# A hybrid decoder block: the inverse joined later, groups begun earlier, first products amid the transposes

## The chip, the cores and the metric

The kernel runs on one core of a Trainium2 chip. The metric is the device time of one execution in microseconds (us). TensorE is PE below, VectorE DVE, ScalarE ACT, GpSimd POOL and SyncE SP.

## The reference, cut to what matters

One layer over 2048 tokens of width 1024, all in float32. Half of the mixing heads are RWKV-7 time mixing (8 heads of 64), the other half differential attention (4 heads); then an output projection, and an MLP with a short causal convolution.

```python
xn = rms_norm(h, ln_attn_pre);  proj = xn @ w_in            # 1792 RWKV and 1536 attention columns
# RWKV, per head: r, k, v, decay, a, g from proj mixed with the token before
kk = k * k_k;  kk = kk / max(norm(kk), 1e-12)               # the key norm
state = state * w + (state @ -kk) (kk * a)^T + v k^T        # token after token
y = state @ r;  y = layer_norm(y + sum(r * k * r_k) * v) * g
o = differential attention of the other columns
h = h + rms_norm(concat(y, o) @ w_out)
h = h + rms_norm((gelu(conv(hn @ w_up)[gate]) * conv(...)[val]) @ w_down)
```

## The kernel before, in words

The run has four stages: projections with the RWKV groups between them; attention; output projection; MLP. The change lies in the first, apart from one buffer count in attention.

**Projections.** The tokens are handled in two halves of 1024, each in two runs `g` of 512. A column block `cb` has 128 columns: 14 blocks for RWKV, 12 for attention. Each float32 operand is split into a high part (rounded) and a low part (the rest), and a product of a block and a run is 24 matmuls of 128x512: three for each of 8 slices of the contraction (L270 to L272). `norm` (L181) loads 128 tokens of x, scales them and stores them as `xn`; `transpose_half` (L85) transposes 512 of their columns on PE (L89), ACT copies the high part (L91) and DVE makes the low part (L92). `start` does this for the first half and then issues the products of blocks 0 and 1. For the second half, `turn` loads `xn` back and transposes it. `plan` yields the other products: blocks 2 to 13 of the first half, then all of the second, then the attention blocks of the first. `evict` writes each product to DRAM, the RWKV blocks as `rw`.

**Pace.** `Pace` is a queue of generators. Each of the 8 steps of a product is one tick, three matmuls; after it, every generator whose tick has come is advanced to its next `yield`, which names the tick, counted from its own start, at which it goes on. So the order on PE is written by hand; inside `manual_schedule` PE's instructions run in the order of the program. The other engines and the DMA queues are ordered by a planner, which runs the program in a modelled time; each engine then runs its list in order.

**A group** (`Rwkv.group`, L449) is 128 tokens of time mixing in two chunks of 64. 16 groups start `PITCH` = 34 ticks apart. In its order:

- Loads by SP; at tick 5 the decay and rate products (L475, L477).
- At 8 the sums of squares of the keys (L492), then `power` (DVE L434, POOL L435); at 13 the eight rows of norms are turned on PE (L441) and split into high and low (L442 on ACT, L443 on DVE); at 16 PE spreads them (L447), and DVE finishes the keys (L518 to L524).
- At 22 and 24 the chunk products `M` (L540, masked by DVE at L543).
- The inverse: M's diagonal 32x32 blocks go to DRAM and back as `ab` (L548, L552), DVE runs 31 steps of two instructions each (L594, L596) on `X`, and X goes through DRAM (`xdr`, L599) to `x1t` (L601), `bdx` and M. `bda` holds M's blocks off the diagonal (L559). At tick `JOIN` = 52 PE joins the blocks: L618 reads `x1t`, L624 `bda`, L628 `bdx`, with an ACT copy after each.
- From `JOIN` + 7 the state: per chunk L643 (state times keys), three ticks later L649, three later L657 to L665, and DVE's update of the state (L662, L663).
- 21 ticks after that the output norm: sums (L675, L682), `power`, turning, spreading, and the gate (L695).

All PE outputs of this stage share 8 PSUM banks in turn.

Of the kernel before, what the change touches and what calls it, by code (L numbers as in the profile page):

```python
# [18 lines left out]
P = 128  # L19
# [3 lines left out]
HALF = 1024  # L23
GRP = 512
NRW = 14
# [9 lines left out]
def load_table(nc, cx, pool, eng, rows, name):  # L35


    tot = sum(r.shape[0] for r in rows)
    st = pool.tile([P, P], F32, name=f"{name}_st", tag=f"tab_st{name}")
    o = 0  # L40
    nc.vector.memset(st, 0.0)
    for r in rows:
        eng.dma_start(st[o:o + r.shape[0], :], r)
        o += r.shape[0]

    def finish():
        pt = cx.ps.tile([P, P], F32, name=f"{name}_ps", tag=cx.mm[0], bufs=cx.mm[1])
        nc.tensor.transpose(pt, st, cx.ident)
        t = cx.const.tile([P, tot], F32, name=name, tag=name)
        nc.vector.tensor_copy(t, pt[:, :tot])  # L50
        return t
    return finish
# [25 lines left out]
def transpose_split(nc, cx, ps, xn, xh, xl, t, tag, bufs):  # L78

    g, o = divmod(t * P, GRP)  # L80
    for hf in range(2):
        transpose_half(nc, cx, ps, xn[:, hf * 512:hf * 512 + 512], xh[g], xl[g], t, hf, o, tag, bufs)
# [75 lines left out]
class Proj:  # L158
# [10 lines left out]
        self.x, self.w = {}, {}  # L169

    def tables(self):
        nc, cx, I = self.nc, self.cx, self.I
        cols = lambda a: a.rearrange("(b p) -> b p", p=P)
        tab = load_table(nc, cx, self.pool, nc.sync, [cols(I["mu_shift"][0]), I["diff_subln"]]
                         + [cols(I[n][0]) for n in self.rk] + [cols(I["r_k"][0].rearrange("h d -> (h d)"))], "chtab")()
        self.mu, cx.subln = tab[:, 0:NRW], tab[:, NRW:NRW + 1]
        cx.rktab = {n: tab[:, NRW + 1 + 4 * i:NRW + 5 + 4 * i] for i, n in enumerate(self.rk + ["r_k"])}
        self.mu1 = cx.const.tile([P, NRW], F32, name="mu1")
        nc.vector.tensor_scalar(self.mu1, self.mu, -1.0, 1.0, op0=ALU.mult, op1=ALU.add)

    def norm(self, t, pool):  # L181

        nc = self.nc
        xt = pool.tile([P, D], F32, name=f"x_{t}", tag="xt", bufs=8)
        nc.sync.dma_start(xt, self.I["x"][0, t * P:(t + 1) * P, :])
        if self.gain is None:
            self.gain = bcast_row(nc, pool, self.I["ln_attn_pre"], D, "g_pre", nc.sync)
        norm_rows(nc, self.cx, pool, xt, xt, self.gain, t)
        nc.sync.dma_start(self.cx.xn[t], xt)
        return xt  # L190

    def alloc(self, half, g):
# [2 lines left out]
        self.x[half, g] = mk("h"), mk("l")  # L195
        return self.x[half, g]

    def start(self, first):

        cx = self.cx  # L200
        xs = [self.alloc(0, g) for g in range(2)]
        for t in range(HALF // P):
            if t == W0:
                self.weights(0, 0)
            if t == TB:
                self.tables()
            transpose_split(self.nc, cx, cx.ps, self.norm(t, first), [x[0] for x in xs], [x[1] for x in xs], t, *cx.ra)
        self.weights(0, 1)
        for g in range(2):
            for cb in range(2):  # L210
                self.product(0, cb, g)
# [113 lines left out]
NC = RG // 64  # L325
MB, SB = 2, 2
ARB = 3
PITCH, JOIN = 34, 52
NGRP = S // RG
DECAY = math.exp(-0.5)  # L330
LN_EPS = 64e-5
# [85 lines left out]
class Rwkv:  # L417
# [20 lines left out]
    def turned(self, bank, sb, rT):  # L438
        nc, cx = self.nc, self.cx
        tp = bank[0:8, 1, :]  # L440
        nc.tensor.transpose(tp, sb, cx.ident)  # L441
        nc.scalar.copy(rT[0:8], tp)  # L442
        nc.vector.tensor_tensor(rT[32:40], tp, rT[0:8].bitcast(F32), op=ALU.subtract)  # L443

    def spread(self, bank, rT):
# [3 lines left out]
    def group(self, g):  # L449
        tc, nc, cx, T, U = self.env(g)  # L450
# [35 lines left out]
        cum = T([P, 4, RG], "t_d")  # L486
        for q in range(2):
            nc.vector.tensor_tensor_scan(flat(cum, q), cx.gate, flat(th, q), 0.0, op0=ALU.mult, op1=ALU.add)
        yield 8
        rn = U([P, 4, RG], "n2")  # L490
        for hb in range(4):
            nc.tensor.matmul(rn[:, 0, 2 * hb:2 * hb + 2], sq[:, hb], cx.ones2c, start=True, stop=True)  # L492
        sb = self.power(rn, ALU.max, 1e-24, f"kk{g}")
        pe, pc = cx.pe, T([P, 4, NC], "pc", 2)
        nc.scalar.activation(pe[:, :, :, 1:65], c4(cum), AF.Exp, scale=-0.5 * DECAY)
        ip = cum
        nc.scalar.activation(ip, cum, AF.Exp, scale=0.5 * DECAY)
# [11 lines left out]
        rk = T([P, 4, RG], "t_b")  # L509
# [3 lines left out]
        self.turned(rn, sb, cx.rT[0])  # L513
        tt(rk, rk, kp, op=ALU.mult)
        tt(rr, pe[:, :, :, 1:65], rr, op=ALU.mult)
        yield 16
        self.spread(rn, cx.rT[0])
        tt(k0, k0, c4(rn), op=ALU.mult)  # L518
        b2 = tha
# [2 lines left out]
            rs = slice(64 * e, 64 * e + 64)  # L522
            tt(BK[rs, :, :, e, :], c4(b2[rs]), c4(ip[rs]), op=ALU.mult)
        tt(k0, pe[:, :, :, 0:64], k0, op=ALU.mult)  # L524
        yield 18
        bo = U([P, 4, RG], "bo")
        nc.tensor.matmul(bo, cx.ones2, rk, start=True, stop=True)
        ybv = T([P, 4, RG], "ybv", 3)
# [3 lines left out]
        M = T([P, NC, 8, P], "M", MB)  # L532
        mk = cx.mask2.unsqueeze(1).broadcast_to([P, 4, P])
        for c in range(NC):
            yield 22 + 2 * c
            se, so = U([P, 4, P], f"se{c}"), U([P, 4, P], f"so{c}")
            for hb in range(4):
                for e, sx in ((0, se), (1, so)):
                    rs = slice(64 * e, 64 * e + 64)
                    nc.tensor.matmul(sx[:, hb, :], BK[rs, hb, c], AR[rs, hb, c], start=True, stop=True)  # L540
            mv = M[:, c].rearrange("p (b e) x -> p e b x", e=2)
            for e, sx in ((0, se), (1, so)):
                tt(mv[:, e], sx, mk, op=ALU.mult)  # L543
        adr = cx.dram.tile([2, 16, 32, 32], F32, name=f"adr_{g}", tag="adr", bufs=2)
        for d in range(2):
            for e in range(2):
                r = 64 * e + 32 * d
# [4 lines left out]
            nc.sync.dma_start(ab[32 * s:32 * s + 32], adr.rearrange("d b j i -> (d b) j i"))  # L552
        X = T([P, 8, 32], "X")
        nc.sync.dma_start(X, cx.xinit)
        mq = M.rearrange("p c (t q) x -> p (c t) q x", q=4)
        for q in range(4):
            qs = slice(32 * q, 32 * q + 32)
            r = 64 * (q % 2)
            nc.sync.dma_start(cx.bda[qs, :, qs], mq[r:r + 32, :, q, 32:64])  # L559
        yield 26  # L560
        sav = T([P, NC, 8, 64], "sav", SB)
        vt = U([P, 4, P], "vt")
        for hb in range(4):
# [4 lines left out]
                               vt[64 * q:64 * q + 64, :, 64 * e:64 * e + 64])  # L568
        bkt = T([P, NC, 512], "bkt", SB)
        for c in range(NC):  # L570
            yield 28 + 2 * c
            bt = U([P, 4, P], f"bt{c}")
            for hb in range(4):
                nc.tensor.transpose(bt[:, hb, :], BK[:, hb, c].rearrange("p a t -> p (a t)"), cx.ident)
            nc.scalar.copy(bkt[:, c, :], bt.rearrange("p h x -> p (h x)"))
# [2 lines left out]
        tmp = T([P, 8 * 16], "xtmp")  # L578
        for j in range(31):
            if j % 5 == 0:  # L580
                yield 32 + 2 * (j // 5)
            if j == 5:
                kv = T([P, NC, 4, 64], "kv", SB)
                wp = U([P, NC, 4, 64], "wp")
                for c in range(NC):
                    for hb in range(4):
                        for e in range(2):
                            h, ks = 2 * hb + e, slice(64 * (1 - e), 64 * (1 - e) + 64)
                            nc.tensor.matmul(wp[64 * e:64 * e + 64, c, hb, :], M[ks, c, h, 0:64], sav[ks, c, h, :],
                                             start=True, stop=True)  # L590
                nc.scalar.copy(kv, wp)
            n, w = j // 4 + 1, 31 - j
            tv = tmp[:, 0:n * w].rearrange("p (n w) -> p n w", w=w)
            tt(tv, X[:, 0:n, j:j + 1].broadcast_to([P, n, w]), ab[:, j:j + 1, j + 1:32].broadcast_to([P, n, w]),  # L594
               op=ALU.mult)
            tt(X[:, 0:n, j + 1:32], X[:, 0:n, j + 1:32], tv, op=ALU.add)  # L596
# [2 lines left out]
            nc.sync.dma_start(xdr.rearrange("d b m s i -> (d b) m s i")[:, :, s, :], X[32 * s:32 * s + 32])  # L599
        x1t = T([P, 16, 32], "x1t")  # L600
        nc.sync.dma_start(x1t[0:32], xdr[0].rearrange("b m s i -> (m s) b i"))  # L601
        xq = xdr[1].rearrange("(t q) m s i -> q (m s) t i", q=4)
        for q in range(4):
            qs = slice(32 * q, 32 * q + 32)
# [146 lines left out]
class Attn:  # L751
# [7 lines left out]
    def T(self, shape, tag, nm, bufs=1, dt=F32):  # L759
        return self.pool.tile(shape, dt, name=f"{tag}_{nm}", tag=tag, bufs=bufs)  # L760
# [32 lines left out]
    def scores(self, h, qb):  # L793
# [10 lines left out]
        n_ = f"{h}_{qb}"  # L804
        ne = (nk + EW - 1) // EW
        E = []
        sc = self.T([P, 16], "asc", n_, 5)
        for c in range(2):
            e = [self.T([P, EW], "E", f"{n_}{c}{i}", EB) for i in range(ne)]
            mx = self.T([P, 8], "amx", f"{n_}{c}", 6)  # L810
# [295 lines left out]
def block_kernel(tc, I, out):  # L1106
    nc = tc.nc
    cx = Ctx()
    with ExitStack() as st:
# [18 lines left out]
        with pool("pj", "left") as pp:  # L1128
            pace = Pace()
            pj = Proj(tc, nc, cx, I, pp, pace)  # L1130
            half = NRW + NDF
            products = pj.plan([(0, range(2, NRW)), (1, range(half)), (0, range(NRW, half))])
            with pool("x0", "right") as xp:
                pj.start(xp)
                for t in range(HALF // P):
                    next(products)
                    pj.norm(HALF // P + t, xp)
            attn_consts(tc, nc, cx, I)
            cx.const = right.enter_context(pool("const2", "right"))
            rwkv_consts(tc, nc, cx, I)  # L1140
            rw = Rwkv(tc, nc, cx, right.enter_context(pool("rk", "right")), cx.ps)
            with tc.manual_schedule(engines={mybir.EngineType.PE}):
                for h, cb, g in products:
                    if (h, cb, g) == (1, 0, 0):
                        for i in range(NGRP):
                            pace.add(rw.group(i), pace.now + 3 + PITCH * i)
                pace.drain()
# [37 lines left out]
```

## Time and profile before

| | us |
|---|---|
| median of 3 runs | 3281.44 |
| lowest, highest | 3276.2, 3283.45 |
| the profiled execution's own time | 3280.6 |
| its span, first to last instruction | 3278.9 |
| PE busy | 3015.5 (92%) |
| DVE busy | 1935.7 (59%) |
| ACT busy | 1175.4 (36%) |
| POOL busy | 436.6 (13%) |

Busy time counts neither waiting nor the issue of DMAs by SP. The profile cuts the span into 40 slices of about 82 us. The granted clock is given as a share of 2.4 GHz; 0.5 is 1.2 GHz. In the waits, the name behind the arrow is what ended the idle time.

### The profile page before, as it was taken

How to read it: one execution, taken by the hardware profiler on the slowest of the kernel's cores; microseconds unless marked ns; L12 is line 12 of the kernel's file. 1: busy time of each engine (PE TensorE's matmuls, PEld its weight loads, DVE VectorE, ACT ScalarE, POOL GpSimd, SP SyncE). 2: the span in 40 equal slices, each digit the busy share in tenths (PEclk: the TensorE clock that was granted, in tenths of full speed). 3: DMA queues.
4: the chain of work that ended last, by engine and by line, in shares of the span. 5: the costliest groups of instructions: out<-in, count | busy, mean ns of one | idle time of the engine just before them, and what ended most of it. 6: DMA issues, size and time to landing. Idle time of an engine off the chain costs nothing.

```text
span 3278.9 us, 46545 instructions
## 1 busy us (share of the span) xinstructions
PE 3015.5 (92%) x17411; PEld 2464.3 (75%) x17411; DVE 1935.7 (59%) x4903; ACT 1175.4 (36%) x2324; POOL 436.6 (13%) x625
## 2 busy tenths in 40 slices
PE   8996887888889869998999999999999999999998
PEld 6874665666667648887788888888888788888886
DVE  6365575574666538777655455555556655555556
ACT  5242332333333237776633422222223422222223
POOL 3211111121221233343100000000000000000002
PEclk9998898998989879999999999999999999999999
DMA  8342232333433383454244311111112411111112
GB/s 295 119 145 71 78 84 75 98 92 92 126 103 97 76 170 66 82 98 99 69 140 166 120 48 51 40 58 46 52 39 94 149 47 51 39 58 46 52 33 84
DMA packets 367074, 290.83 MB, mean 89 GB/s; under 512 B 114511, under 2 KB 317874, under 8 KB 366850
## 3 DMA queue, kind: packets, MB, share of 16 engines
q1 hardware_dynamic: 327858, 219.85, 22.6%
q0 software_dynamic: 36688, 63.82, 8.7%
q10 hardware_dynamic: 2304, 4.20, 0.3%
q8 instruction: 138, 2.26, 0.3%
q14 instruction: 86, 0.70, 0.1%
HBM read 208.91 MB, written 78.07 MB: 88 GB/s over the span
## 4 chain that ended last, share of the span: by engine, by line
PE 71%; DVE 11%; DMA 7%; issue 5%; SPq 2%; POOL 2%; ACT 1%; DVEq 0%; POOLq 0%; ACTq 0%
PE fp L103 10%; PE fp L104 10%; PE fp L105 10%; PE dn L104 5%; PE dn L103 5%; PE dn L105 5%; PE op L860 3%; PE pp L270 3%; PE pp L271 2%; PE pp L272 2%; DVE X L596 2%; DVE xtmp L594 2%; PE po L103 2%; PE po L105 2%; PE po L104 2%
## 5 line engine op out<-in xcount | busy, mean ns | idle before, releaser
L1043 DVE TENSOR_TENSOR acc<-dn,acc 128x512 f32<-128x512 f32 x320 | 211.3, 686 | 224.6 <-PE dn L105 222.1
L103 PE MATMUL fp<-f1h,uh 128*128 128x512 f32 x704 | 276.2, 393 | 4.0 <-DVE fcarry L1008 4.0
L104 PE MATMUL fp<-f1l,uh 128*128 128x512 f32 x704 | 275.9, 392 | 0.0
L105 PE MATMUL fp<-f1h,ul 128*128 128x512 f32 x704 | 275.5, 391 | 0.0
L104 PE MATMUL dn<-dl,gh 128*128 128x512 f32 x704 | 275.3, 391 | 0.0
L103 PE MATMUL fp<-f0h,uh 128*128 128x512 f32 x704 | 274.2, 390 | 0.0
L105 PE MATMUL fp<-f0h,ul 128*128 128x512 f32 x704 | 274.2, 390 | 0.0
L103 PE MATMUL dn<-dh,gh 128*128 128x512 f32 x704 | 272.5, 391 | 1.9 <-DVE acc L1043 1.9
L104 PE MATMUL fp<-f0l,uh 128*128 128x512 f32 x704 | 274.1, 389 | 0.0
L105 PE MATMUL dn<-dh,gl 128*128 128x512 f32 x704 | 263.9, 391 | 0.0
L97 DVE TENSOR_TENSOR ul<-ur,uh 128x1024 fp32r<-128x1024 f32 x88 | 107.7, 1225 | 188.5 <-ACT uh L96 188.5
L821 DVE TENSOR_SCALAR_CACHE_REDUCE E<-sp 128x512 f32<-128x512 f32 (+3 forms) x320 | 184.8, 605 | 54.0 <-PE sp L819 32.6
L1004 DVE SCALAR_TENSOR_TENSOR u<-fp,cvA,u 128x511 f32<-128x511 f32 x176 | 131.2, 746 | 119.9 <-ACT u L1002 119.9
L96 ACT CAST dh<-dr 128x1024 fp32r<-128x1024 f32 x44 | 44.4, 1047 | 386.8 <-PE dn L105 384.0
L860 PE MATMUL op<-V,at 128*128 128x128 f32 x1088 | 156.2, 286 | 12.0 <-ACT at L856 11.8
L816 PE MATMUL sp<-ka,qa 128*128 128x512 f32 (+3 forms) x320 | 137.4, 441 | 27.7 <-DMA qa<-qq 19.6
L860 PEld LDWEIGHTS op<-V,at 128*128 128x128 f32 x1088 | 143.9, 198 | 23.9 <-ACT at L856 18.2
L594 DVE TENSOR_TENSOR xtmp<-X,ab 128x60 f32<-128x60 f32 (+24 forms) x496 | 111.0, 224 | 84.6 <-DMA ab<-adr 72.4
L830 ACT ACTIVATE E<-E,asc 128x1024 f32<-128x1024 f32 (+7 forms) x160 | 153.5, 965 | 14.7 <-DVE asc L826 14.7
L1002 ACT ACTIVATE u<-fp,cvB 128x512 f32<-128x512 f32 x176 | 136.4, 776 | 60.4 <-PE fp L105 60.3
L103 PEld LDWEIGHTS fp<-f1h,uh 128*128 128x128 f32 x704 | 133.2, 189 | 32.4 <-issue 4.4
L103 PEld LDWEIGHTS dn<-dh,gh 128*128 128x128 f32 x704 | 132.5, 188 | 30.2 <-DVE acc L1043 2.3
(343 smaller groups left out, 7057.8 us busy)
## 6 DMA issues: line engine op xcount, KB each, us to landing
ur<-in_w_up SPq DMA_DIRECT2D x88, 512.0 KB
wr<-in_w_in SPq DMA_DIRECT2D x52, 512.0 KB
dr<-in_w_down SPq DMA_DIRECT2D x44, 512.0 KB
rw<-e POOLq DMA_DIRECT2D x56, 256.0 KB, 2.5
x<-in_x SPq DMA_DIRECT2D x16, 512.0 KB
xn<-x SPq DMA_DIRECT2D x16, 512.0 KB
xr<-xn SPq DMA_DIRECT2D x32, 256.0 KB
ab<-adr SPq DMA_DIRECT2D x64, 128.0 KB
```

The lines of the kernel that those rows point to most:

```text
L97: nc.vector.tensor_tensor(wl, wr, wh.bitcast(F32), op=ALU.subtract)
L103: nc.tensor.matmul(out, lh(kb), rh(kb), start=(kb == 0), stop=False)
L104: nc.tensor.matmul(out, lh(kb), rl(kb), start=False, stop=False)
L105: nc.tensor.matmul(out, ll(kb), rh(kb), start=False, stop=(kb == n - 1))
L594: tt(tv, X[:, 0:n, j:j + 1].broadcast_to([P, n, w]), ab[:, j:j + 1, j + 1:32].broadcast_to([P, n, w]), op=ALU.mult)
L816: nc.tensor.matmul(sp[:, 0:n], qa[:, c, qs], ka[:, c, 0:n], start=True, stop=False)
L821: nc.vector.tensor_scalar(e[ch * GRP // EW][:, eo:eo + n], sp[:, 0:n], -1.0, None, op0=ALU.mult, op1=ALU.min, accum_out=mx[:, ch:ch + 1])
L830: nc.scalar.activation(e[i][:, 0:n], e[i][:, 0:n], AF.Exp, bias=nm, scale=-1.0, accum_out=z)
L860: nc.tensor.matmul(op, at[:, q, :], v[:, q, :], start=(kb == 0), stop=(kb == qb))
L1002: nc.scalar.activation(u, pp, AF.Identity, bias=wb(b), scale=w2(b))
L1004: stt(u[:, 1:GRP], pp[:, 0:GRP - 1], w1(b), u[:, 1:GRP], op0=ALU.mult, op1=ALU.add)
L1043: nc.vector.tensor_tensor(acc[:, t, ds_], po, acc[:, t, ds_], op=ALU.add)
```

## The change

`JOIN` becomes 64. In the group the sums of squares come at tick 7, the spreading at 17, `bo` at 20, `M` at 24 and 26, and all steps up to the inverse two ticks later than before. The copy of the turned row moves from ACT to DVE. `bda` is loaded after the load of `x1t` is issued. The groups are put in the queue before the product of the last RWKV block and the second run, two products earlier. `start` transposes four of the eight rows of tokens, issues the products, and lets the queue do the rest of the transposes (`rest`) and the turning of the table (`tab`) between their matmuls; the weights of block 1 are loaded earlier, and `xn` is stored from POOL's queue. PE's order by hand now begins with `start`.

```diff
@@ Proj.tables, named
-        tab = load_table(..., "chtab")()
+        fin = load_table(..., "chtab")
+        def end():
+            self.named(fin())
+            yield from ()
+        return end()
+    def named(self, tab):
@@ Proj.norm
-        nc.sync.dma_start(self.cx.xn[t], xt)
+        nc.gpsimd.dma_start(self.cx.xn[t], xt)
@@ Proj.start
+    def rows(self, t, hf, xn, x):
+        transpose_half(self.nc, self.cx, self.cx.ps, xn[:, hf * 512:hf * 512 + 512], *x, t, hf, t * P % GRP, *self.cx.ra)
...
             if t == TB:
-                self.tables()
-            transpose_split(self.nc, cx, cx.ps, self.norm(t, first), [x[0] for x in xs], [x[1] for x in xs], t, *cx.ra)
-        self.weights(0, 1)
+                tab = self.tables()
+                self.weights(0, 1)
+            xt.append(self.norm(t, first))
+            if t < 4:
+                for hf in range(2):
+                    self.rows(t, hf, xt[t], xs[0])
+        def rest():
+            for i in range(8):
+                t, hf = 4 + i // 2, i % 2
+                self.rows(t, hf, xt[t], xs[1])
+                yield 1 + 2 * i
+        self.pace.add(tab, 6)
+        self.pace.add(rest(), 1)
@@ Rwkv
-PITCH, JOIN = 34, 52
+PITCH, JOIN = 34, 64
-        nc.scalar.copy(rT[0:8], tp)
+        nc.vector.tensor_copy(rT[0:8], tp)
-        yield 8
+        yield 7
-        pe, pc = cx.pe, T([P, 4, NC], "pc", 2)
+        pe, pc = cx.pe, T([P, 4, NC], "pc", 3)
-        yield 16
+        yield 17
-        yield 18
+        yield 20
-            yield 22 + 2 * c
+            yield 24 + 2 * c
-        yield 26
+        yield 28
...
-            yield 28 + 2 * c
+            yield 30 + 2 * c
-                yield 32 + 2 * (j // 5)
+                yield 34 + 2 * (j // 5)
         nc.sync.dma_start(x1t[0:32], xdr[0].rearrange("b m s i -> (m s) b i"))
+        mq = M.rearrange("p c (t q) x -> p (c t) q x", q=4)
+        for q in range(4):
+            qs = slice(32 * q, 32 * q + 32)
+            r = 64 * (q % 2)
+            nc.sync.dma_start(cx.bda[qs, :, qs], mq[r:r + 32, :, q, 32:64])
@@ Attn.scores
-        sc = self.T([P, 16], "asc", n_, 5)
+        sc = self.T([P, 16], "asc", n_, 4)
@@ block_kernel (pj.start and all products now inside manual_schedule)
-                    if (h, cb, g) == (1, 0, 0):
+                    if at == (0, NRW - 1, 1):
```

## Rows read from the trace of the kernel before

**Rows 1.** The page: TensorE's granted clock in 40 slices, tenths of full speed.

```profile
PEclk9998898998989879999999999999999999999999
```

**Rows 2.** Waits of PE, 150 to 1190 us: total us, times, longest us.

```profile
PE xp L618 <- DMA x1t<-xdr: 130.9, 16, 15.1
PE n L441 <- POOL rs_kk L435: 17.2, 15, 2.7
...
PE rp L643 <- DVE xtmp L594: 3.3, 3, 1.5
```

**Rows 3.** Windows of one stall: each engine's busy us; near the end the clock.

```profile
619.80:629.00 9.20, 0.01 (x1) 0.01 (x1) 3.03 (x8) 0.00 (x0) 2.12 (x2) 0.68 0.41 107
629.00:633.40 4.40, 4.40 (x11) 2.92 (x12) 0.69 (x1) 0.27 (x1) 0.00 (x0) 0.50 0.37 70
633.40:677.60 44.20, 43.06 (x402) 34.14 (x401) 30.59 (x93) 17.02 (x36) 10.75 (x14) 1.00 0.36 99
```

**Rows 4.** Windows of 10.2 us after each stall, first and last of sixteen.

```profile
267.00:277.20 10.20, 10.18 (x54) 7.58 (x55) 1.98 (x3) 1.25 (x4) 0.00 (x0) 0.78 0.17 31
...
1137.50:1147.70 10.20, 10.18 (x46) 7.90 (x46) 1.54 (x3) 2.11 (x6) 2.17 (x4) 0.78 0.31 68
```

**Rows 5.** Timeline of PE, 629 to 687 us: start us, us, instruction, idle before.

```profile
632.28 0.63 PE L272 MATMUL pp<-x3h,wl 128*128 128x512 f32 x1
632.71 0.63 PE L270 MATMUL pp<-x3h,wh 128*128 128x512 f32 x1
...
635.66 0.39 PE L271 MATMUL pp<-x3l,wh 128*128 128x512 f32 x1
635.89 0.40 PE L272 MATMUL pp<-x3h,wl 128*128 128x512 f32 x1
...
665.76 0.95 PE L492 MATMUL n<-ones2c,t_a 128*128 128x2 f32 x8
...
671.91 0.27 PE L441 MATMUL n<-ident,rs_kk 128*8 128x128 f32 x1 [0.78 <-POOL rs_kk L435]
...
686.55 0.60 PE L618 MATMUL xp<-ident,x1t 32*128 32x32 f32 x4 [8.90 <-DMA x1t<-xdr]
```

**Rows 6.** Timeline of DVE, 642 to 681 us: last M, inverse's ends.

```profile
642.13 0.68 DVE L543 TENSOR_TENSOR M<-so,mask 128x512 f32<-128x512 f32 x1
...
649.83 0.19 DVE L594 TENSOR_TENSOR xtmp<-X,ab 128x31 f32<-128x31 f32 x1 [4.97 <-DMA ab<-adr]
...
680.17 0.17 DVE L596 TENSOR_TENSOR X<-X,xtmp 128x8 f32<-128x8 f32 x1
```

**Rows 7.** Tile xp, the joining's transposes: ns min/median/max, first and last start.

```profile
L618 PE MATMUL xp<-ident,x1t x64: 214/289/311, 267.0 to 1137.8; 32*128 32x32 f32 x64
```

**Rows 8.** Timeline of PE at 267 us, the first group's joining.

```profile
267.02 0.52 PE L618 MATMUL xp<-ident,x1t 32*128 32x32 f32 x3 [15.08 <-DMA x1t<-xdr]
```

**Rows 9.** Timeline of DVE at 225 us, the first group's last M.

```profile
224.58 0.68 DVE L543 TENSOR_TENSOR M<-so,mask 128x512 f32<-128x512 f32 x1
```

**Rows 10.** Windows: fifteen pitches; one inverse; the time after it. DVE is third.

```profile
267.00:1137.50 870.50, 728.29 (x6202) 566.04 (x6203) 522.28 (x1576) 271.15 (x564) 160.05 (x203) 0.91 0.35 91
649.80:680.40 30.60, 26.71 (x265) 21.06 (x263) 28.57 (x92) 9.97 (x20) 10.78 (x13) 1.00 0.41 117
680.40:709.00 28.60, 22.45 (x178) 17.16 (x180) 7.89 (x13) 8.56 (x20) 4.20 (x8) 0.82 0.34 73
```

**Rows 11.** Waits of DVE, whole run.

```profile
DVE xtmp L594 <- DMA ab<-adr: 72.4, 16, 8.0
```

**Rows 12.** Windows: the head, PE first, POOL fifth, then clock and DMA share.

```profile
0.00:30.50 30.50, 14.16 (x65) 11.89 (x66) 21.51 (x44) 23.21 (x55) 7.14 (x15) 0.92 0.90 321
```

**Rows 13.** Timeline of DVE, head: the fourth row's second split.

```profile
23.98 0.68 DVE L92 TENSOR_TENSOR x1l<-xt,x1h 128x512 fp32r<-128x512 f32 x1
```

**Rows 14.** Timeline of PE, head.

```profile
24.14 1.06 PE L89 MATMUL xt<-ident,x 128*128 128x128 f32 x8 [1.33 <-DVE n_ss L62]
```

**Rows 15.** Waits of SP's DMA queue, whole run.

```profile
SPq L232 <- DVE X L596: 43.6, 9, 18.6
```

More of the change, by code (lines that the diff above doesn't have):

```diff
@@ L173, in tables @@
         cols = lambda a: a.rearrange("(b p) -> b p", p=P)
-        tab = load_table(nc, cx, self.pool, nc.sync, [cols(I["mu_shift"][0]), I["diff_subln"]]
-                         + [cols(I[n][0]) for n in self.rk] + [cols(I["r_k"][0].rearrange("h d -> (h d)"))], "chtab")()
+        fin = load_table(nc, cx, self.pool, nc.sync, [cols(I["mu_shift"][0]), I["diff_subln"]]
+                         + [cols(I[n][0]) for n in self.rk] + [cols(I["r_k"][0].rearrange("h d -> (h d)"))], "chtab")
+        def end():
[3 more added lines that the diff above has]
+    def named(self, tab):
+        nc, cx = self.nc, self.cx
         self.mu, cx.subln = tab[:, 0:NRW], tab[:, NRW:NRW + 1]
@@ L196, in alloc @@
         return self.x[half, g]
+    def rows(self, t, hf, xn, x):
+        transpose_half(self.nc, self.cx, self.cx.ps, xn[:, hf * 512:hf * 512 + 512], *x, t, hf, t * P % GRP, *self.cx.ra)
     def start(self, first):
-        cx = self.cx
         xs = [self.alloc(0, g) for g in range(2)]
+        xt = []
         for t in range(HALF // P):
@@ L554, in group @@
         nc.sync.dma_start(X, cx.xinit)
[L555 to L559, printed above, removed]
-        yield 26
+        yield 28
         sav = T([P, NC, 8, 64], "sav", SB)
@@ L1132, in block_kernel @@
             products = pj.plan([(0, range(2, NRW)), (1, range(half)), (0, range(NRW, half))])
[L1133 to L1141, printed above, removed]
-            with tc.manual_schedule(engines={mybir.EngineType.PE}):
-                for h, cb, g in products:
-                    if (h, cb, g) == (1, 0, 0):
+            with tc.manual_schedule(engines={mybir.EngineType.PE}):
+                with pool("x0", "right") as xp:
+                    pj.start(xp)
+                    for t in range(HALF // P):
+                        next(products)
+                        pj.norm(HALF // P + t, xp)
+                attn_consts(tc, nc, cx, I)
+                cx.const = right.enter_context(pool("const2", "right"))
+                rwkv_consts(tc, nc, cx, I)
+                rw = Rwkv(tc, nc, cx, right.enter_context(pool("rk", "right")), cx.ps)
+                for at in products:
+                    if at == (0, NRW - 1, 1):
                         for i in range(NGRP):
```

## The prediction

> **What bounds the kernel now.** I read the page first, then the tables of windows, the waits of PE, and the timelines of one group. The granted clock by slices [rows 1] is above nine tenths from slice 16 on and dips again and again in slices 4 to 15. Here, roughly from 150 to 1190 us, the RWKV groups run beside the projections; the start of attention is the lowest, slice 15. Later stages (attention, output projection, MLP) the change touches only by one buffer of a 16-column tile, so the forecast is made in this stretch.
>
> TensorE's waits there [rows 2] have one giant: the transposes at L618, the first instructions of the joining of the inverse, stand 130.9 us for the DMA of `x1t`, 16 times, once per group, 15.1 us at most. Everything else is small: the key norm's turned row at L441 17.2 us in 15 waits, the state product at L643 3.3 us in its largest entry. PE's order is written by hand here, so nothing behind L618 can run while it waits.
>
> A second loss hangs on the same wait. In one of them [rows 3] the 9.20 us stall ran at a mean granted clock of 0.68, the 4.40 us after it at 0.50 (1.2 GHz), and the next 44.20 us at 1.00 (2.4 GHz). In the 10.2 us that follow each of the sixteen stalls the granted clock is 0.72 on average; the first and the last of the sixteen windows stand in [rows 4], both at 0.78. A deficit of 0.28 between two levels means that 0.56 of that time, 5.7 us, is at half speed: 16 x 5.7 = 92 us. Projection matmuls follow each other every 0.43 us at half speed (632.28 to 632.71) and every 0.23 us at full speed (635.66 to 635.89) [rows 5]. So the loss is 92 x (1 - 0.23/0.43) = 43 us.
>
> Why L618 waits: in the group of 629 to 687 us [rows 6] the last product M ends at 642.8; the first step of the inverse starts at 649.83 (DVE stood 4.97 us for `ab`), its last ends at 680.3, and PE gets `x1t` at 686.55 after a wait of 8.90 [rows 5]. That is 43.8 us from M to the joining, of which 30.5 us are the DVE steps. The rest is DMA, before and after.
>
> **The change part by part.**
>
> *The joining, 52 to 64, M two ticks later.* Before, M's last products stand at tick 24 and the joining at 52: 28 ticks. After: 26 and 64, so 38. The first joining of the sixteen starts at 267.0, the last at 1137.5 (the last of its four at 1137.8, [rows 7]), 15 pitches of 58.0 us. Less the stalls (115.8 of the 130.9 us, without the first, so 7.7 each), half-speed (2.7) and the other waits (about 1.5), a pitch is 46.1 us of PE work for 34 ticks, 1.36 us per tick. 38 ticks are 51.5 us, against the 43.8 needed: the wait goes. Not in the first group: there M ended at 225.3 [rows 9] and PE arrived at 267.0 - 15.1 = 251.9 [rows 8], 26.6 us for 28 sparse ticks or 0.95 each. Ten more bring 10 to 11 of the missing 15.1; about 4 us stay. Gain 130.9 - 4 = 127. Bounds: 131, and half of it (65) if the chain itself grows (rival 2).
>
> *Clock.* With the long stalls gone the half-speed stretches behind them go: 43, less 2 for the first group's remainder, so 41. Bounds 0 and 43.
>
> *Key norm.* Its sums come at tick 7 instead of 8 and the turning stays at 13: six ticks instead of five. In [rows 5] the sums start at 665.76 and the turning at 671.91 after a wait of 0.78, so five ticks were 5.4 us. One bare tick is three matmuls, 0.69 us, and the new neighbours in these ticks (output and state products of an older group, ticks 9 and 12) add some more. Waits average 17.2/15 = 1.15, so most of them end: I take 12 of 17.2, bounds 5 and 17. The spreading moves from 16 to 17 and the copy of the row from ACT to DVE: one crossing between engines less, one DVE copy of 8x128 more. I cost this at nothing, hidden in the four ticks that the pair now has; uncovered it would be a small DVE step like the 0.19 us one in [rows 6], twice a group, 6 us in all.
>
> *More groups alive; `pc` 3 buffers, `asc` 4, `bda` written later.* A group now lives 105 ticks, three pitches and three ticks. Counted by ticks, `AR` (3 buffers) is last read at 86 and rewritten at 102, M (2) at 86 and 92, `ybv` at 105 and 122: no new wait on these. `bda` would have been overwritten at 24 + 34 = 58 while still read at 66, hence its move behind the load of `x1t`. On SP's queue four issues go from before `ab`'s end to behind `x1t`; what is behind them (`bdx`, M's blocks) is read four or more ticks after the joining's first step. Zero; bounds -5 and +10.
>
> *New waits.* This is the uncertain part. In the group above DVE is busy 28.57 of 30.60 us while the inverse runs and 7.89 of 28.60 outside [rows 10]; over all pitches 522.28 of 870.50, 34.8 us per pitch. A pitch of 48 us puts DVE at 73%: it isn't the bound, but it loses the rest that the stalls gave it. Two sets of steps move from DVE's idle part into or against its full part. First, the output norm: its turned row now comes at 33 modulo 34, five ticks after its sums at 28, and at that time DVE stands before `ab` (72.4 us in 16 waits, [rows 11]), in order, with the norm's small step possibly behind. Second, the first state product of a group moves from 25 to 3 and its update from 31 to 9, among the scans and key products. Bounds: nothing, and the longest key-norm wait, 2.7 us, at one place in each group plus 10 for the state, 53. I take the nearest rows [rows 2]: the output norm like the key norm today, 17, and the state steps at four times their largest entry of 3.3, 13. Sum 30.
>
> *The groups start two products (16 ticks) sooner.* The groups take 3 + 15 x 34 + 105 = 618 ticks instead of 606, inside 624 instead of 608. PE's work is the same and the last step stays inside the last product: zero. The first group's loads now share SP's queue with the loads for the second half's transposes: 0 to +5.
>
> *Head.* `start` now transposes four rows of x, and does the other eight halves inside the first two products. Before, PE began its products at 30.5 us, after all transposes; until then it was busy 14.16 of 30.50 us [rows 12]. But the fourth row's second split ends only at 24.66 on DVE [rows 13], and from 24.14 to 30.5 PE did transposes, which remain to be done. What vanishes are PE's short waits there: the first, 1.33 us, stands in [rows 14], and two after it are smaller. I take 3 for all; bounds -3 (the hand-written order makes PE wait where it could choose) and 8. In that window the DMA engines are busy 0.90 of the time [rows 12]. The stores of xn move from SP to POOL's queue: I cost that at nothing, because POOL has 7.14 busy in 30.5 us. The Trainium skill, page "DMA: Bandwidth & Descriptors", section "Issuing engines are not separate DMA queues", says that all queues feed the same 16 engines and another issuer saves issue time only. By that rule the head gains the 3 us and nothing from the move; if instead the loads came sooner by it, the head would be at its bound of 8 and the sum 5 lower.
>
> **Sum.** The profiled execution took 3280.6 us (span 3278.9 and 1.7 around it), 0.8 below the median of 3281.4. 3280.6 - 127 - 41 - 12 - 3 + 30 = 3127.6. I predict 3128.
>
> **Rivals.**
> 1. *All of it, and no new wait.* 3127.6 - 30 - 5 (rest of the key norm) = 3093, at the bounds of the first group and the head 3082. For: PE and DVE ran in step through 44.20 us with 43.06 busy [rows 3], while DVE was full. Against: each pitch had a stall in which DVE caught up.
> 2. *The inverse gets longer.* Its steps are a chain on DVE with other work between; a denser pitch could put more between. If a mean of 4 us per joining stays, 60 more of the wait and 20 of the half-speed stay, while new waits halve (DVE catches up again): 3128 + 60 + 20 - 15 = 3193. For: the needed time varies; 43.8 us leaves less than 8 of slack. Against: the inverse lies across nearly the same steps as before.
> 3. *Slower.* SP issues in order, and weight loads (L232) stood behind the inverse's end up to 18.6 us [rows 15]. If such a load comes late for its product, PE stops for it. The price per group is the stop plus the 2.7 us of half speed; slower than before by over 0.2% (3288) from 160/16 = 10 us per group, a stop of 7.3. With 12 us: 3128 + 16 x 14.7 = 3363. Against: in the view of [rows 2] no projection product waits, and weights are doubly buffered.
> 4. *The waits go, the half-speed stays:* 3128 + 41 = 3169. TensorE's rows speak against it: the clock was 1.00 over 44.20 us with a wait of 0.78 inside [rows 3, 5]. The Trainium skill, page "TensorE: Matmul & The Clock Gate", section "A second HAM failure mode: psum-queue depth-cycling", tells of a kernel whose many short idles between matmul groups kept the clock swinging. By that rule the new short waits would keep it low; the trace doesn't agree so far.
> 5. *It doesn't do what it says:* every step of the inverse, loads included, shifts with the joining, and the wait is as before: 3281.
>
> **Chances.** Forecast (3100 to 3155) 0.46, rival 1 0.24, rival 2 0.17, rival 4 0.05; these four are faster, 0.92. Rival 5 0.03 is the same (within 0.2%, about what a measurement of this kernel tells from no change). Rival 3 0.05 is slower. From 3078 to 3198 holds the forecast, rival 4, and most of rivals 1 and 2.
>
> **What would show it.** In PE's waits of the changed kernel L618's counterpart should have one wait of some us, the first group's, instead of sixteen. The granted clock should be at or near 1.00 from 300 to 1000 us. Joinings should come every 47 to 49 us instead of 58. The key norm's wait should be 5 us in all, and the output norm's L441 and L643 should appear with 10 to 40. The first product should start near 25 us. Wrong would be: waits over 3 us on `x1t` in most groups (rival 2), PE waiting for weights (rival 3), clock dips without long waits (rival 4).

## The result and the profile after

| | before | after |
|---|---|---|
| median us (4 runs each) | 3279.57 | 3187.55 |
| lowest, highest | 3276.2, 3283.45 | 3179.7, 3195.13 |
| span of the profiled execution | 3278.9 | 3189.3 |
| mean granted clock over the span | 0.956 | 0.972 |

The changed kernel is faster: 0.9719 of the time before (95% interval 0.969 to 0.9747). It lies inside the range of 3078 to 3198, but 60 us above the 3128 forecast; of the gain of 153 us that the sum had, 92 came.

The page's slices of the granted clock, of the kernel after, for [rows 1]:

```profile
PEclk9998999999999889999999999999999999999999
```

Counted from 1, the row of dips in slices 4 to 14 has become one dip in slice 4 and nines from 5 to 13. Attention's start, 7 and 9 in slices 15 and 16 before, reads 8 and 8 in slices 14 and 15. PE's waits from 150 to 1090 us, for [rows 2] (total us, times, longest us; the transposes of `x1t` are now at L641, the state product at L666, the spreading at L470):

```profile
PE vs L470 <- DVE rT L466: 22.6, 8, 4.3
PE rp L666 <- DVE X L614: 11.1, 7, 3.4
PE xp L641 <- DMA x1t<-xdr: 11.0, 1, 11.0
PE xt L89 <- DMA xr<-xn: 8.1, 4, 4.5
PE rp L666 <- DVE xtmp L612: 5.0, 4, 2.3
```

`x1t` is waited for once, in the first group, instead of 16 times: 130.9 us became 11.0. The key norm's turned row, 17.2 us before, is gone from the whole list, of which these are the five largest. New at the top is the spreading of the output norm, which stands for DVE. For [rows 7], the first and the last joining:

```profile
L641 PE MATMUL xp<-ident,x1t x64: 221/222/291, 267.9 to 1039.3; 32*128 32x32 f32 x64
```

The last of its four begins at 1039.3, the last joining at 1039.1: the pitch is (1039.1 - 267.9)/15 = 51.4 us, against 58.0 before and the 47 to 49 of the forecast.

Where the time came from is read by windows: first the stage from product 24 to the last product, then attention. The columns are those of [rows 3]: start, end and length; busy us and instructions of PE, of its weight loads, of DVE, ACT and POOL; then granted clock, DMA share and GB/s. Of the kernel before:

```profile
162.20:1183.60 1021.40, 857.09 (x7009) 667.59 (x7007) 599.95 (x1764) 320.15 (x654) 187.24 (x241) 0.91 0.35 94
1183.60:1613.30 429.70, 372.57 (x2530) 322.61 (x2529) 317.73 (x1164) 304.80 (x773) 158.82 (x240) 0.91 0.49 96
```

Of the kernel after:

```profile
160.50:1086.00 925.50, 854.00 (x7009) 665.90 (x7007) 601.56 (x1801) 311.25 (x623) 195.31 (x243) 0.95 0.40 104
1086.00:1525.20 439.20, 381.28 (x2529) 323.84 (x2529) 318.35 (x1161) 308.19 (x773) 157.46 (x239) 0.92 0.48 94
```

The span fell by 89.6 us: 1.7 up to product 24, 95.9 in the stage, 1.5 in output projection and MLP, while attention took 9.5 more. In the stage PE's idle time fell from 164.3 to 71.5 us. The same 7009 matmuls took 857.1 us and take 854.0: PE's busy time gave back 3 us, where the forecast had 41 from the clock.

One new wait in three windows (wait, what follows, rest of the pitch), and the same kernel after a shorter one:

```profile
376.30:379.50 3.20, 0.00 (x0) 0.00 (x0) 1.89 (x10) 0.00 (x0) 0.00 (x0) 0.99 0.06 11
379.50:386.20 6.70, 6.64 (x60) 5.54 (x61) 4.90 (x22) 2.12 (x5) 0.00 (x0) 0.50 0.00 0
386.20:432.20 46.00, 42.54 (x355) 32.85 (x354) 30.14 (x87) 17.01 (x32) 8.46 (x8) 1.00 0.37 100
...
690.90:694.50 3.60, 3.56 (x58) 2.94 (x59) 3.28 (x14) 0.62 (x2) 1.03 (x2) 1.00 0.41 91
```

The clock is 0.99 while PE stands and 0.50 for the 6.7 us after: a wait of 3.3 us is followed by no less half speed than the sixteen waits before, where 5.7 us on average [rows 4] stood behind 8.2. After 2.28 us of waiting at 690.9 it stayed at 1.00. Between 300 and 1040 us there are ten such dips, of 3.4 to 6.8 us, each with a wait of 2.34 to 4.51 us, 3.3 on average.

What made that wait, on DVE (start, duration; in brackets the idle time before and what ended it):

```profile
370.58 0.16 DVE L278 COPY carry<-pp 128x1 f32<-128x1 f32 x1
377.37 0.19 DVE L612 TENSOR_TENSOR xtmp<-X,ab 128x31 f32<-128x31 f32 x1 [6.63 <-DMA ab<-adr]
378.82 0.27 DVE L465 CAST rT<-vs 8x128 fp32r<-8x128 f32 x1
379.22 0.28 DVE L466 TENSOR_TENSOR rT<-vs,rT 8x128 fp32r<-8x128 f32 x1
```

and on PE:

```profile
372.71 0.27 PE L464 MATMUL vs<-ident,rs_ln 128*8 128x128 f32 x1
379.56 0.68 PE L470 MATMUL vs<-rT,sel 40*128 40x128 f32 x2 [3.29 <-DVE rT L466]
```

PE turned the norms at 372.7. DVE was idle then, standing for `ab` since 370.7, with the row's copy (L465) listed behind the inverse's first seven instructions, of which the first is shown. DVE runs its list in order, so the copy came at 378.8, and PE stood. SP is one reason why `ab` comes late. M ends at 418.55 in the next group, and SP's queue goes on so:

```profile
418.54 1.91 SPq L628 DMA_DIRECT2D bdx<-xdr  x4
420.49 2.88 SPq L632 DMA_DIRECT2D M<-xdr  x4
423.47 1.87 SPq L571 DMA_DIRECT2D adr<-M  x4
```

M's blocks leave 4.9 us after M's end, behind two sets of loads of the group before. Over the stage, the waits of DVE for `ab`, and those of SP's queue before it can load the gate's tile `sg` (L696), which the gate product (L718) has still to read (140 to 1100 us):

```profile
DVE xtmp L612 <- DMA ab<-adr: 80.3, 12, 10.9
...
SPq L696 <- PE gp L718: 82.1, 13, 13.2
```

### The profile page after: what moved, and what is told of

It reads as the page before. It is cut to its first block, busy times and chain, and to the rows that moved or that the text cites. A ratio compares the mean times of both kernels' runs of the same rounds, so it can differ in the third digit from the quotient of the medians.

```text
span 3189.3 us, 46522 instructions
## 1 busy us (share of the span) xinstructions
PE 3016.8 (95%) x17411; PEld 2459.6 (77%) x17411; DVE 1937.6 (61%) x4935; ACT 1168.1 (37%) x2292; POOL 448.9 (14%) x641
## 4 chain that ended last, share of the span: by engine, by line
PE 70%; DVE 10%; issue 7%; DMA 6%; ACT 2%; SPq 2%; POOL 2%; DVEq 0%; POOLq 0%; ACTq 0%
PE fp L103 10%; PE fp L105 10%; PE fp L104 10%; PE dn L104 5%; PE dn L103 5%; PE dn L105 5%; PE pp L293 3%; PE op L883 3%; PE pp L294 2%; PE pp L295 2%; PE po L103 2%; PE po L105 2%; PE po L104 2%; DVE xtmp L612 1%; DVE X L614 1%
```

## The experiments

Ratios are to the kernel before, run on the same chip, with 95% intervals.

**a_join52: the joining alone taken back.**

```diff
-PITCH, JOIN = 34, 64
+PITCH, JOIN = 34, 52
```

> The changed kernel with the joining put back from tick 64 to 52, all else as changed. My theory, that the later joining carries the gain: M comes two ticks later than in the kernel before, so the slack is 26 ticks instead of 28; the wait on x1t is back in all sixteen groups with 130 to 180 us in sum, the clock dips behind each, and the time is 3270 to 3320 us, no better than before. Rival, that the other edits (key norm, start, earlier groups) carry it: under 3230 us.

Measured: 3336.63 us, 1.017 (1.0151 to 1.0189). Its waits of PE, 150 to 1245 us:

```profile
PE xp L641 <- DMA x1t<-xdr: 183.7, 16, 17.1
PE n L464 <- POOL rs_kk L458: 9.1, 11, 1.1
```

All sixteen waits for `x1t` are back, and 3.3 us each longer than before: M stays two ticks later, 2.7 us at 1.36 us per tick. Without the joining the rest of the change is a loss, 53 us of it in these waits. The time is above the expected one.

**b_onlyjoin: the kernel before with `JOIN` 64 and what that needs.**

```diff
-PITCH, JOIN = 34, 52
+PITCH, JOIN = 34, 64
-        pe, pc = cx.pe, T([P, 4, NC], "pc", 2)
+        pe, pc = cx.pe, T([P, 4, NC], "pc", 3)
-        sc = self.T([P, 16], "asc", n_, 5)
+        sc = self.T([P, 16], "asc", n_, 4)
...
+            nc.sync.dma_start(cx.bda[qs, :, qs], mq[r:r + 32, :, q, 32:64])
```

(The last line is moved behind the load of `x1t`, as in the change.)

> The kernel before with the joining at 64 alone, and what it needs (pc in 3 buffers, asc in 4, bda loaded behind x1t). My theory: x1t is waited for in the first group at most; the key norm's wait at L441 stays near 17 us; the time is 3185 to 3215 us, so that this one edit has over four fifths of the 92 us. Rival, that the other edits carry a good part: over 3230 us.

Measured: 3178.96 us, 0.9683 (0.9661 to 0.9706). PE's waits, 150 to 1090 us:

```profile
PE vs L447 <- DVE rT L443: 17.4, 10, 3.1
PE rp L643 <- DVE X L591: 13.6, 7, 4.0
...
PE xp L618 <- DMA x1t<-xdr: 7.8, 1, 7.8
PE n L441 <- POOL rs_kk L435: 3.1, 1, 3.1
```

These edits give the whole gain. The key norm's wait, 17.2 us in 15 before, is 3.1 in 1 though its ticks are as before: my theory that it needed its own edit is wrong. Most of it went with the old joining; a_join52 has the old joining with the new ticks, and there 9.1 us in 11 stay. The new waits come with the new one: the same two places head the list.

**c_sg2: the gate's tile with two buffers, so that SP needn't stand for it.** (`on`, of attention, gives the room.)

```diff
-        sg = T([P, RG], "sg")
+        sg = T([P, RG], "sg", 2)
-        on = self.T([P, P], "on", n_, 6)
+        on = self.T([P, P], "on", n_, 5)
```

> The changed kernel with two buffers for sg (and on in 5 instead of 6, for space). In the changed kernel SP stands 82 us for the gate product before it can load sg, and the stores of M stand behind it, up to 5 us after M is there. My theory, that this makes ab late, so that DVE stands for ab with the turned row behind it, and PE for that row: SP's stand there goes, M's stores are issued within 1.5 us of M, PE's wait for the turned row falls to under 12 us, and the time is 3165 to 3178 us. Rival, SP's stand hurts nobody because the inverse has slack: 3183 to 3192 us and the same wait of PE.

Measured: 3180.5 us, 0.9695 (0.9676 to 0.9714), an interval that overlaps that of the change. SP's waits, 140 to 1100 us, then PE's, 150 to 1090:

```profile
SPq L696 <- PE gp L718: 65.4, 13, 10.2
```

```profile
PE vs L470 <- DVE rT L466: 18.1, 7, 3.4
```

SP's stand shrank by 17 us and didn't go; PE's by 4.5. A second buffer is no cure, and a gain of 7 us can't be told from none; the wait missed the expected 12, the time the expected 3178.

**d_spread3: the output norm's spreading three ticks later.**

```diff
-        yield at + 12
+        yield at + 15
-        yield at + 13
+        yield at + 16
```

> The changed kernel with the spreading of the output norm's row three ticks later (and the gate behind it). My theory, that waits of 2 to 4 us cost twice, once as waits and once by the half-speed clock behind them: the 22.6 us that PE stood for the turned row fall under 5, the eight clock dips behind them go too, and the time is 3150 to 3165 us, more gained than the waits themselves. Rival 1, dips have another cause: about 3167 us, the dips stay. Rival 2, PE stands for DVE at the next step instead: 3180 us or more.

Measured: 3193.33 us, 0.9731 (0.9711 to 0.9751), no gain. PE's waits, 150 to 1090 us:

```profile
PE rp L666 <- DVE X L614: 21.3, 6, 4.8
PE rp L666 <- DVE xtmp L612: 11.3, 5, 4.0
```

The spreading no longer waits, and the next PE step that needs DVE stands instead: 16.1 us in these two rows in the change, 32.6 here. PE's idle time in the stage is 69.5 us against 71.5. The forecast missed, the rival held: DVE's stand is passed on to whoever comes next.

**e_asc4: the kernel before with `asc` in 4 buffers, nothing else.**

```diff
-        sc = self.T([P, 16], "asc", n_, 5)
+        sc = self.T([P, 16], "asc", n_, 4)
```

> The kernel before with asc in 4 buffers instead of 5 and nothing else. In the changed kernel attention takes 439 us from the end of the groups to its last output product, before 430, although no wait there grew; the order of PE and DVE in attention differs between the two. My theory, that the fourth buffer alone makes the planner order attention otherwise: attention 436 to 441 us, the first stage as before, 3286 to 3292 us in all. Rival, that attention loses by the state in which it starts (loads, clock): attention 430 us, 3277 to 3283 us.

Measured: 3299.11 us (6 runs), 1.0054 (1.0034 to 1.0074): slower by about half a per cent, and above the expected time. Its two windows, the stage of the groups and attention:

```profile
162.10:1193.60 1031.50, 869.53 (x7009) 676.38 (x7007) 600.00 (x1764) 320.36 (x654) 188.62 (x241) 0.90 0.35 93
1193.60:1638.60 445.00, 380.64 (x2530) 322.67 (x2529) 319.77 (x1164) 307.22 (x773) 158.14 (x240) 0.92 0.49 94
```

Attention took 445.0 us against 429.7: the same 2530 matmuls are busy 8 us longer and the idle time grew by 7. One wait of DVE there is the buffer's own, the first write to `asc` (L826) behind its last reader:

```profile
DVE asc L826 <- POOL on L867: 4.9, 5, 1.3
```

It was 0.7 us in 1 before; in the change it is 5.4 in 6, and 0.7 in 1 again in k_after_asc5. The order of PE's and DVE's instructions in attention is also another one, since the planner lays it out by when buffers come free; which share is whose was not taken apart. In this execution the stage of the groups was longer too, 1031.5 us against 1021.4, though every engine's order up to attention is that of the kernel before. PE's idle time there is no longer (162.0 us against 164.3). The time at half speed with PE busy is: 123.5 us against 95.0, and PE's busy time is 12.4 us longer.

**g_head: the change with its head undone** (all transposes first, the table in line, `xn` stored by SP).

```diff
-        nc.gpsimd.dma_start(self.cx.xn[t], xt)
+        nc.sync.dma_start(self.cx.xn[t], xt)
...
-        self.pace.add(tab, 6)
-        self.pace.add(rest(), 1)
...
+        self.weights(0, 1)
```

> The changed kernel with its head put back: all transposes of the first half before the products, the table in line, xn stored by SP. My theory, that the head is worth 0 to 3 us because the first weights of the next block and the second run's splits end at the same time either way: 3187 to 3192 us, and the first stage's products 0 to 3 us later from the ninth on. Rival 1, the head gains the 6 us by which the first product starts earlier: 3193 or more. Rival 2, it costs, being part of why the joining alone is quicker than the whole change: under 3184.

Measured: 3172.95 us, 0.9669 (0.9653 to 0.9685), 14.6 less than the change. The head itself isn't where it is: the fifth product starts at 51.5 us in it and at 51.7 in the change. The stage after it is 907.4 us against 925.5, with 65.6 idle on PE against 71.5 and 44.5 us of half speed with PE busy against 71.4. A second pair, below, shows no such price.

**h_late: the groups begun where they were.**

```diff
-                    if at == (0, NRW - 1, 1):
+                    if at == (1, 0, 0):
```

> The changed kernel with the groups begun with the second half's first product again, 16 ticks later. My theory, that starting earlier puts the first group's loads into the stretch in which SP and the DMA engines serve the second half's transposes, and gives a tail without products in return: the tail after the last product is 10 ticks of group steps, some 8 to 12 us, the beginning gains as much, 3183 to 3192 us. Rival, that the early start costs more than it saves (the joining alone is quicker than the whole change): under 3180 us. Rival 2, that it saves: over 3195 us.

Measured: 3187.09 us, 0.9721 (0.9702 to 0.974). The earlier groups are worth nothing, as the forecast's zero had it.

**i_asc5: b_onlyjoin with `asc` back at 5.**

```diff
-        sc = self.T([P, 16], "asc", n_, 4)
+        sc = self.T([P, 16], "asc", n_, 5)
-        on = self.T([P, P], "on", n_, 6)
+        on = self.T([P, P], "on", n_, 5)
```

> The kernel before with the joining at 64 alone, asc kept at 5 buffers (on in 5 instead of 6, for space). My theory: attention is back at 430 us and the run 8 to 10 us shorter than with asc in 4, 3167 to 3173 us. Rival (the start state): 3175 to 3182 us, attention at 439.

Measured: 3163.44 us, 0.9638 (0.9621 to 0.9655). Attention:

```profile
1072.40:1498.80 426.40, 373.01 (x2530) 324.40 (x2528) 320.40 (x1164) 305.66 (x774) 153.63 (x234) 0.91 0.49 95
```

13.1 us less in attention than in b_onlyjoin (439.5). That `on` at 5 isn't the cause shows in c_sg2, which has it with `asc` 4: 437.0. This kernel, the later joining and little else, is faster than before and than the change (whose interval begins at 0.969).

**k_after_asc5 and j_best: the change, and the change without its head, each with `asc` 5 and `on` 5** (the same two lines as in i_asc5).

> The whole changed kernel with asc in 5 buffers (on in 5, for space). If the asc edit costs in the change what it costs alone: attention 426 to 432 us instead of 439 and 3168 to 3178 us. Rival, that it costs only beside the order of the kernel before: attention 437 us or more, 3183 to 3192 us.

> The changed kernel without its head edits and with asc in 5 buffers (on in 5, for space): the joining at 64, the ticks of the key norm, the copy on DVE and the earlier groups are left. If the prices found so far add up (head 14.6, asc 15.5): 3187.5 - 14.6 - 15.5 = 3157 us, 3152 to 3163, and 6 less than the joining alone with asc in 5 (3163). Rival, that the prices are luck of the order that the planner finds and don't add: 3163 to 3180 us.

Measured: 3169.33 us, 0.9667 (0.9648 to 0.9686), and 3167.83 us, 0.9663 (0.9641 to 0.9686). Attention of k_after_asc5:

```profile
1077.20:1502.10 424.90, 368.84 (x2529) 319.82 (x2529) 316.38 (x1161) 305.11 (x773) 157.83 (x239) 0.92 0.50 97
```

439.2 became 424.9, so `asc` costs the change 14 us there and 18 in all. But the head's price doesn't add: 1.5 us between these two, 14.6 between the change and g_head; j_best missed its 3157, and its rival held. Neither beats i_asc5: head, key-norm ticks, DVE's copy and earlier groups together gain nothing.

**m_act: j_best with M's blocks sent and `ab` loaded from ACT's queue, past SP's.**

```diff
-                nc.sync.dma_start(adr[d].rearrange("(b e) j i -> e j b i", e=2)[e],
+                nc.scalar.dma_start(adr[d].rearrange("(b e) j i -> e j b i", e=2)[e],
...
-            nc.sync.dma_start(ab[32 * s:32 * s + 32], adr.rearrange("d b j i -> (d b) j i"))
+            nc.scalar.dma_start(ab[32 * s:32 * s + 32], adr.rearrange("d b j i -> (d b) j i"))
```

> As the kernel above without head edits and with asc in 5, but M's stores to adr and the loads of ab are issued from ACT's queue instead of SP's. My theory, that PE's waits for the output norm's row come from DVE standing for an ab that is late because its DMAs stand in SP's queue: M's stores are issued within 1 us of M, DVE's stand for ab falls from 75 to 100 us to under 55, PE's wait for the row to under 8, and the time is 8 to 20 us below the kernel above. Rival 1, the stand is DMA time and not the queue: it stays over 70 us and the time within 5 us. Rival 2, ACT stands for M and holds back PE's copies: slower.

Measured: 3165.08 us, 0.9647 (0.9628 to 0.9667). Waits of DVE in j_best, then in m_act, then of PE in j_best and in m_act (all 150 to 1090 us):

```profile
DVE xtmp L603 <- DMA ab<-adr: 81.7, 13, 10.6
```

```profile
DVE xtmp L603 <- DMA ab<-adr: 55.5, 12, 10.4
```

```profile
PE vs L461 <- DVE rT L457: 19.9, 7, 4.8
```

```profile
PE xp L638 <- ACT x L633: 20.7, 10, 4.3
```

Before the longest of the last, which ends at 725.17, on ACT:

```profile
723.08 1.74 ACTq L566 DMA_DIRECT2D ab<-adr  x4
724.86 0.27 ACT L633 COPY x<-xp 128x128 f32<-128x128 f32 x1 [4.09 <-issue]
```

SP's queue was a third of DVE's stand (26 of 82 us), and the spreading's wait is gone with it. As much waiting came back at the joining, whose copies ACT makes in order behind its new DMA work. The time is the same within the intervals; the expected 8 to 20 us did not come. The Trainium skill, page "DMA: Bandwidth & Descriptors", section "Issuing engines are not separate DMA queues", says that another issuer saves only the sequencer's time to initiate a DMA, which is usually small beside the DMA itself; here the saving was 26 us on DVE, from a queue that stands, and the time agrees with the rule all the same.

**p_join60: j_best joined at 60.**

```diff
-PITCH, JOIN = 34, 64
+PITCH, JOIN = 34, 60
```

> As the kernel without head edits and with asc in 5, with the joining at 60 instead of 64. By the slack of the prediction, 34 ticks of 1.36 us are 46 us, against 43.8 needed and up to 4 more where SP issues M's stores late: waits on x1t come back in most groups, 0 to 5 us each, 20 to 50 in sum, and the time is 20 to 50 us longer than at 64. Rival, that 60 is enough and the turned row of the output norm now comes before DVE stands for ab: no waits on x1t but the first group's, and the time the same or shorter.

Measured: 3166.1 us, 0.965 (0.9629 to 0.9672); expected was a loss of 20 to 50. PE's waits, 150 to 1090 us:

```profile
PE xp L632 <- DMA x1t<-xdr: 35.0, 9, 12.7
```

The wait for `x1t` came back in nine groups as forecast, and the spreading's 19.9 us are off the list. PE's idle time in the stage is 72.3 us against 64.7 in j_best, and its time the same. Between 60 and 64 the waits only change places.

## Why the prediction was right, and where its size was off

**The wait at the joining (forecast -127): right.** 120 us went. In the first group 11.0 us stayed, not 4. The ticks were as long as forecast: M ended at 218.59 and PE came to the joining at 267.9 - 11.0 = 256.9, 38.3 us later, against 26.6 before [rows 8, 9]. The chain itself grew, from 41.8 to 49.3 us, which is rival 2 in this one group. DVE of the kernel after, then of before:

```profile
217.91 0.68 DVE L566 TENSOR_TENSOR M<-so,mask 128x512 f32<-128x512 f32 x1
226.40 0.19 DVE L612 TENSOR_TENSOR xtmp<-X,ab 128x31 f32<-128x31 f32 x1 [4.46 <-DMA ab<-adr]
259.69 0.17 DVE L614 TENSOR_TENSOR X<-X,xtmp 128x8 f32<-128x8 f32 x1
```

```profile
233.20 0.19 DVE L594 TENSOR_TENSOR xtmp<-X,ab 128x31 f32<-128x31 f32 x1 [2.48 <-DMA ab<-adr]
260.80 0.17 DVE L596 TENSOR_TENSOR X<-X,xtmp 128x8 f32<-128x8 f32 x1
```

The inverse took 33.5 us instead of 27.8: between its steps DVE did 20.1 us of other work, against 14.1 before. M of the next group is among it, whose products PE now reaches before the joining. b_onlyjoin and a_join52 show from both sides that this edit carries the gain.

**Half-speed clock (forecast -41): the term that failed.** Its step was "With the long stalls gone the half-speed stretches behind them go". Ten of them came back, with waits that were on average less than half as long; the granted clock from 300 to 1000 us, forecast at or near 1.00, was 0.97 (0.90 before). In the stage the time at half speed with PE busy fell from 95 to 71 us (the clock's record laid over PE's busy time), which at the forecast's own rate of 1 - 0.23/0.43 is 11 us; PE's busy time shows 3, and the other 8 are not explained. So 30 to 38 us of the 60 that are missing lie here. That rate itself is borne out by e_asc4: 28.5 us more at half speed made PE's busy time 12.4 us longer, 0.44 each against 0.47. The forecast priced each new wait by its length alone and gave the clock back whole. Rival 4 had the price, 3169, and too small a chance: it rested on one window of 44.20 us with a wait of 0.78 in it [rows 3, 5], which says nothing of waits of 2 to 4 us. The Trainium skill's page "TensorE: Matmul & The Clock Gate", section "A second HAM failure mode: psum-queue depth-cycling", was weighed there and put aside; the trace of after agrees with it, as far as short idles between matmuls keep the clock swinging.

**Key norm (-12): the wait went, for another reason.** All of the 17.2 us; by b_onlyjoin 14 go without any edit to the key norm, and by a_join52 8 go with the edits and the old joining.

**New waits (+30): right in place, too small.** The output norm and the state product, as named; 22.6 us at the norm instead of 17, some 44 in all with the smaller entries (stage idle 71.5, less the 11.0 of the first joining and 16 of entries that were there before). DVE's in-order stand for `ab` was named too, but its sum was taken from the key norm's waits, which had no such stand.

**`asc` (zero, bounds -5 and +10): wrong and outside its bounds.** 13 to 15 us in attention and 15 to 19 in the time: e_asc4 against the kernel before, the change against k_after_asc5, b_onlyjoin against i_asc5. I had put it with the edits of the groups, without following the tile in attention: its last reader (POOL's `on`) is late enough for the next write to wait, and the planner writes another order around it.

**Head (-3) and earlier groups (0).** The first product starts at 24.0 us instead of 30.5, as forecast:

```profile
24.00 0.79 PE L293 MATMUL pp<-x1h,wh 128*128 128x512 f32 x1 [2.75 <-ACT x1h L91]
```

The transposes left to do eat it: by product 24 nothing can be seen of it. Kernels with the head start that product at 160.5 to 161.9 us, those without it at 160.3 to 162.3.

**Rivals.** Rival 1 fell: in no experiment is PE's idle time in the stage under 61 us. Rival 2 fell as a price, not as a mechanism: from M's end to the load of `x1t` it took 46.9 us on average instead of 41.1, but the new slack held that in every group but the first. With the joining at 60 (p_join60) it did not in nine. Rivals 3 and 5 fell: no weight is waited for, and the wait went.

**What was luck.** Four terms were too good by 7 (first group), 30 to 38 (clock), 14 (new waits) and some 15 us (`asc`), while the key norm gave 5 more than forecast. The time is inside the range because the range was wide, not because the sum was right.

**Open.** Why the head costs 14.6 us in one pair and 1.5 in the other. The stage of the change and of k_after_asc5, with the same planned order up to attention, took 925.5 and 915.7 us in their profiled executions, so one profile of this stage can't tell differences under 10 us. Of `asc`, how much is the wait and how much the order.

## What to carry to other kernels

When one long wait is removed from a hand-ordered engine, the engines that caught up in it lose their rest: look for the in-order stand (here DVE before `ab`) that has small steps listed behind it, and price its waits with the half speed that follows them. Removing that stand's victims one by one moves the wait to the next (d_spread3, m_act, p_join60). A buffer count can be an edit of the order where a planner lays out the program, as `asc` was here, so time it by itself.

## What the runs showed of the hardware

The length of the wait does not settle whether the clock falls. In i_asc5, two starts behind a wait:

```profile
759.45 0.68 PE L643 MATMUL rp<-state,AR 64*64 64x64 f32 x16 [3.15 <-DVE X L591]
...
854.00 1.11 PE L447 MATMUL vs<-rT,sel 40*128 40x128 f32 x4 [2.87 <-DVE rT L443]
```

and the 3 us after each:

```profile
759.40:762.40 3.00, 2.95 (x26) 2.19 (x26) 2.47 (x12) 0.79 (x2) 0.00 (x0) 1.00 0.30 88
854.00:857.00 3.00, 3.00 (x14) 2.13 (x15) 2.62 (x12) 0.00 (x0) 0.01 (x1) 0.50 0.37 78
```

The longer wait left the clock at 2.4 GHz, the shorter one was followed by 1.2 GHz. The projection matmuls behind them follow each other every 0.23 us (760.40 to 760.63) and every 0.43 us (855.63 to 856.06); the counts (26 and 14) are of different matmuls. In the changed kernel all ten waits of 2.34 us or more between 300 and 1040 us had their dip and the one of 2.28 us had none, but one of 2.21 us, at 296.3, had one; in i_asc5, with about as much idle time (70.6 us), the time at half speed with PE busy was 39 us against 71. What else decides was not tried.

The clock also differs between executions of one program, and the time with it. The four of the changed kernel had mean granted clocks of 0.971 to 0.976 and took 3195.1 to 3179.7 us. An estimate: 0.005 of 3190 us is 16 us of full speed, so 32 us at half speed, and at the rate of 0.47 that is 15 us, the 15.4 measured. In e_asc4 and the kernel before, the stage of the groups, with one order of instructions, differs by 10 us in the same way.
